# Token blocks of 768, 768 and 576 with seven products in the first two, the low parts of the weights on one engine by kind, and a longer lag before the stores

## The chip, the cores and the metric

The kernel runs on one core of one Trainium2 chip. The metric is the device time of one execution in microseconds, median over the runs. The core has a matrix engine (PE, whose weight loads are shown as PEld), a vector engine (VectorE, DVE in the profile), an activation engine (ScalarE, ACT), a general engine (GpSimd, POOL) and a synchronization engine (SyncE, SP), which issues nearly all DMA transfers. Each engine works off its own instructions in the order in which the program gives them to it; between engines they are held together by semaphores.

## What is computed

One layer of a streaming encoder over 2048 prompt tokens and 64 sample tokens, each a row of 1024 floats, in float32:

```python
h = rms_norm(x, norm1_g) * (1 + sc1) + sh1
z = h @ w_in                       # conv pair | q | k | v | two gates
conv_out = conv_module(...)        # depthwise, 31 taps, LayerNorm, projection
attn_out = attend(q, k, v) @ w_attn_out
merged = sigmoid(g_conv) * conv_out + sigmoid(g_attn) * attn_out
x = x + gt1 * (merged @ w_o)
h2 = rms_norm(x, norm2_g) * (1 + sc2) + sh2
gate, up = split(h2 @ w_ffn_in)    # 1024 -> 2 x 2816
x = x + gt2 * ((silu(gate) * up) @ w_ffn_out)
```

The prompt and the sample have their own conditioning, so their own shifts, scales and gates (`gt1`, `gt2`).

## The kernel before

**Products.** A float32 product is made of three matmuls. Each operand x is kept as two tiles, a high part (x copied to the matrix engine's reduced float type) and a low part (x minus the high part); the matmuls are high by high, high by low, low by high. For every weight tile that comes from memory ACT writes the high part (`whi`), and a subtraction `wlo<-...,whi` writes the low part. That subtraction is on VectorE or on GpSimd: `Weights.split` chooses (lines 458 to 460). Before the change the down weights, the up weights and the merge's weights go to GpSimd, unless the planner's own clock for GpSimd runs more than `BEHIND` = 4000 ns ahead of its clock for PE; then VectorE gets it. Of `w_o` every second slab is always VectorE's.

**Stages.** Up to about 1226 us the kernel makes the projections, the convolution and the attention, in four blocks of tokens (`PBLOCKS`), and leaves conv and attention outputs and the gates in DRAM (`c_d`, `o_d`, `g_d`). What follows runs once for each block of `CBLOCKS`, a loop that starts at line 1720. Before, the blocks have 576, 768 and 768 tokens; the sample's 64 tokens are the first tile of block 0. A block has these steps:

- the merge: the two projections of `c_d` and `o_d` (weights of the kind "ca"), multiplied by the gates, in two chunks of columns;
- `w_o`, the residual `x1`, its norm (`residual`, line 1630: the factor `r` is a power on GpSimd, then ACT scales the row, PE transposes it), and from its columns the operand tiles of the up projection (`t1` to `t4`, `b11` to `b22`, written by VectorE);
- the up projection, `up`, line 1924, over 22 slices f of 128 hidden columns. It works on 2 by 2 blocks (two halves of the contraction, two halves of the tokens) by Winograd's scheme: seven products in place of eight, where sums of weight quarters (`s1` to `s4`, and the plain ones `a11`, `a12`, `a22`) meet sums of token quarters. The first slices are begun earlier with "fi" weights, while the norm is still under way (tile `early`);
- the down projection, accumulated in token rows `acc`; block 0 does it plainly (eight products, "fo" weights, two slices at a time), blocks 1 and 2 do the pairs f = 4, 6, ..., 18 (`PAIRS`) with seven products ("dn" weights, sums T1 to T4 of `w_ffn_out` rows). In up() a callback `at` puts the slabs of a pair of the down projection between those of the next pair of the up projection; `dn_at` says where;
- the end of the block: the last two slices of the down projection for all tiles, multiplied by `gt2` and added to `x1`, then stored. The rows `x1` come from DRAM again (`x<-x_d`).

The sums `s1` to `s4` are made once, in block 0, by GpSimd (`ws<-...`), and are stored to `sum_d`; blocks 1 and 2 load them. Likewise the first block with "dn" makes their sums and their high and low parts and stores these; the other one loads them.

**What sets the order.** The program is written by a planner. Every instruction that passes `Meter.run` (line 104, so nearly all instructions show L104) adds an estimated time to its engine's clock in the planner; generators of side work (weight loads, residuals, stores) are stepped when their due time has come. The order on each engine is thereby fixed in advance, and a store of an output is emitted `OUT_LAG` = 4000 ns after the planner's time of the instruction that wrote it (line 2019). Weights wait in pools: five slabs of `whi` and `wlo` (`held`), three staging tiles `wst`, one `wup`, two `wfo`, four `ws` for sums. In PSUM there are four banks of the tag "y" and four of "gp", of which the down projection's `pd` takes two at a time.

Of the kernel before, what the change touches and what calls it, by code (L numbers as in the profile page):

```python
# [35 lines left out]
CBLOCKS = [(0, 576), (576, 1344), (1344, 2112)]  # L36
# [14 lines left out]
OUT_LAG = 4000.0  # L51
# [28 lines left out]
def tile_chunks(lo, hi):  # L80

    tiles = token_tiles(lo, hi)
    t, n = tiles[(len(tiles) + 1) // 2 - 1]
    return [(lo, t + n), (t + n, hi)]
# [168 lines left out]
class Weights:  # L253
# [5 lines left out]
    def __init__(self, tc, engines, pool, dram, stream, keys, source, staging, held, kept):  # L259
# [17 lines left out]
        for i, key in enumerate(keys):  # L277
            n = times[key] = times.get(key, 0) + 1
            if key[0] == "dn" and n == 1:
# [85 lines left out]
    def kind(key):  # L365
        return "fo" if key[0] in ("fo", "fr") else ""

    def free_tag(self, kind, sure=True):

        tags = self.tags[kind]  # L370
        if kind == "fo" and (self.items[self.due["fo"][0]][0] == "fr" or any(self.items[i][0] == "fi" for i in self.due[""])):
            tags = tags[:1]
# [17 lines left out]
    def load_on(self, kind):  # L390
        while self.due[kind] and self.free_tag(kind):
            self.load(kind)
# [48 lines left out]
    def split(self):  # L441
# [17 lines left out]
        if name == "pool" and self.sum_pool and self.stream.load["pool"] - self.stream.load["pe"] > BEHIND:  # L459
# [81 lines left out]
def up_operands(f):  # L541
# [3 lines left out]
    ops = (["s2", "s3", "s1"] if f else ["s3", "s2", "s1"]) + ["a12"] * (f >= EARLY) + ["a22"] + ["a11"] * (EARLY <= f + 1 < NF) + ["s4"]  # L545
# [3 lines left out]
def dn_at(f):  # L549

    return (0, 1, 3, 6 if f == PAIRS[-1] else 4)
# [8 lines left out]
def weight_order():  # L560
# [10 lines left out]
    for s, (lo, hi) in enumerate(CBLOCKS):  # L571
# [4 lines left out]
        for f in range(0, NF, 2):  # L576
            ops = up_operands(f) + up_operands(f + 1)
            for j in range(0, len(ops), 2):
                yield ("up", *ops[j : j + 2])
                if s and f - 2 in PAIRS:  # L580
# [4 lines left out]
        yield from (("fo", f) for f in range(NF - 2 if s else NF - 4, NF))  # L585
# [3 lines left out]
def streaming_layer(ctx: ExitStack, tc: tile.TileContext, I, O):  # L589
# [479 lines left out]
    def gate_columns(c0, c1, ct):  # L1069
        g = [half_piece(ct % 2, "tg") for _ in range(2)]  # L1070
        for j in range(2):
            nc.sync.dma_start(g[j][:, : c1 - c0], g_d[j, ct, :, c0:c1])
        return g

    def load_mixed(c0, c1, i):

        src = [[quarter("cin", i) for _ in range(2)] for _ in range(2)]
        for j, a in enumerate((c_d, o_d)):
            for l in range(2):
                nc.sync.dma_start(src[l][j][:, :, : c1 - c0].bitcast(F32), a[l, :, :, c0:c1].rearrange("c p t -> p c t"))  # L1080
# [549 lines left out]
    def residual(pp, t, n, gt1, a, half, hs, free, last):  # L1630


        which = int(t < SMP)
        x_t = [wk.tile([P, 512], F32, tag="ws", name="x_t", bufs=4) for _ in range(2)]
        for j in range(2):
            nc.sync.dma_start(x_t[j][:n], rows(x_p, x_s, t, n)[:, 512 * j : 512 * j + 512])
# [83 lines left out]
    for s, (lo, hi) in enumerate(CBLOCKS):  # L1720
        tiles = token_tiles(lo, hi)
        half = (hi - lo) // 2
        gt1, groups, hs = {}, [], None
        chunks = tile_chunks(lo, hi)
        for i, (c0, c1) in enumerate(chunks):
# [8 lines left out]
            if not groups:  # L1734
                for which in {int(t < SMP) for t, _ in tiles}:
# [39 lines left out]
        hid = [wk.tile([P, 2, 2, CW] if not s else [P, 4, 2, CW // 2], F32R, tag="m0", name="hid"), None]  # L1775
# [40 lines left out]
        def rows_of(f, t, n):  # L1816

            if s:
# [5 lines left out]
        def hidden(f, i, ps):  # L1824
            if s:
# [98 lines left out]
        def up(f, ops, at):  # L1924
# [27 lines left out]
            rest_of_late()  # L1952
            if f % 2 == 0:
                at(0)
            step(y, "s1", "t1", False, False)
            plus(v, y, v)
            if f % 2:
                at(4)
            if f >= EARLY:
                x = bank("gp")  # L1960
                step(x, "a12", "b21", True, True)
                plus(x, x, s1)
                silu(c1, x)
            if f % 2 == 0:
# [3 lines left out]
            two = s and f - f % 2 in PAIRS  # L1968
# [15 lines left out]
        def down(fs, ws):  # L1984

            last = fs[-1] == NF - 1
            for i, (t, n) in enumerate(tiles):
# [3 lines left out]
                gt = gt2[int(t < SMP)] if last else None  # L1991
# [12 lines left out]
                for j, ps in enumerate(pss):  # L2004
# [7 lines left out]
                    else:  # L2012
                        if not final:
                            dve.tensor_tensor(ps[:n], ps[:n], dst, ALU.add)
                        dve.tensor_tensor(ps[:n], ps[:n], gt[:n, f], ALU.mult)
                        dve.tensor_tensor(dst, ps[:n], dst if final else x1[j], ALU.add)
                        stream.at(
                            stream.when("dve") + OUT_LAG,
                            lambda t=t, n=n, f=f, dst=dst: nc.sync.dma_start(rows(y_p, y_s, t, n)[:, f], dst),
# [27 lines left out]
        if not s:  # L2047
            W.open("fo", "wfo")
        turns.drain()
# [3 lines left out]
        for f in range(0, NF, 2):  # L2053
            ops = Operands(f)
            if s and f == PAIRS[0]:
                hid[1] = wk.tile([P, 4, 2, CW // 2], F32R, tag="m1", name="hid")
            elif not s and f // 2 % 2 and f >= NF - 4:
                hid[1] = wk.tile([P, 2, 2, CW], F32R, tag="m1", name="hid")

            def at(i, f=f):  # L2060
                if s and f - 2 in PAIRS:
# [10 lines left out]
        end = NF - 2 if s else NF - 4  # L2072
        ws = [W.get(("fo", f)) for f in range(end, NF)]
        gt2 = {which: gt_row(1, which) for which in {int(t < SMP) for t, _ in tiles}}
# [39 lines left out]
```

## Time and profile before

| what | value |
|---|---|
| median of 3 runs | 3046.8 us (3046.7 to 3047.27) |
| the profiled execution's own time | 3042.59 us |
| its span | 3040.8 us |
| DVE busy | 2052.4 us, 67% |
| ACT busy | 1256.8 us, 41% |
| GpSimd (POOL) busy | 985.3 us, 32% |
| instructions | 44889 |
| DMA moved | 690.98 MB, mean 227 GB/s |

The busy shares are means over a long program with unlike stages, so the prediction cuts the span into stretches: the first 1226 us; block 0's start (1226 to 1430), its steady part (1430 to 1726) and its end with block 1's start (1726 to 1946); block 1's steady part (1946 to 2366); its end with block 2's start (2366 to 2566); block 2's steady part (2566 to 3005) and the tail. In rows of groups, "a<-b,c 128x512 x42 | 50.8, 1211" is an instruction that writes tile a from tiles b and c, its shape, its count, the busy time in us and the mean time of one in ns; behind the second bar stands the engine's idle time just before, and what ended it. In rows of the timeline the first two numbers are the start and the duration in us, and a bracket holds the idle time before and its releaser.

### The profile page before, as it was taken

To read this page: it belongs to the slowest core of one execution; us is meant where nothing else is said; L and a number is where in the kernel's file an instruction comes from. 1 tells how busy PE (TensorE), PEld (TensorE's weight loads), DVE (VectorE), ACT (ScalarE), POOL (GpSimd) and SP (SyncE) were. 2 spreads that over 40 slices of the span, in tenths; PEclk is the share of its full clock that TensorE was granted. 3 is DMA by queue.
4 is the path that set the end of the run, shared out by engine and by line. 5 is a ranking of instruction groups with operands and counts; after the bars stand their busy time and mean duration, and the time that the engine had idled before them with its cause. 6 is when DMAs were issued, how large, how long until landed. Compare 5 with 4: busy or idle time off the path is not lost. (4 is left out here: it accounts for less than half of the span.)

```text
span 3040.8 us, 44889 instructions
## 1 busy us (share of the span) xinstructions
PE 2934.8 (97%) x16259; PEld 2606.5 (86%) x16259; DVE 2052.4 (67%) x3835; ACT 1256.8 (41%) x2267; POOL 985.3 (32%) x617
## 2 busy tenths in 40 slices
PE   7989898999999999989999999999999999999998
PEld 4889776888888788878989889999999898999997
DVE  5896678777977895467666755655666756366567
ACT  3324532453254257464444425534444244333332
POOL 1200120101011102355677433247767341333331
PEclk9999998999999999999999999999999999999999
DMA  9888788888997788886444786455556965355554
GB/s 305 268 275 299 230 286 278 275 263 268 305 284 243 247 265 282 253 285 215 149 143 144 231 290 207 157 165 190 182 194 201 342 215 190 118 167 173 166 160 176
DMA packets 487019, 690.98 MB, mean 227 GB/s; under 512 B 38420, under 2 KB 316808, under 8 KB 486797
## 3 DMA queue, kind: packets, MB, share of 16 engines
q1 hardware_dynamic: 474517, 670.72, 67.3%
q10 hardware_dynamic: 12280, 17.39, 1.6%
q8 instruction: 128, 2.10, 0.3%
q14 instruction: 94, 0.77, 0.1%
HBM read 503.79 MB, written 184.19 MB: 226 GB/s over the span
## 5 line engine op out<-in xcount | busy, mean ns | idle before, releaser
L104 POOL TENSOR_TENSOR wlo<-wst,whi 128x1024 fp32r<-128x1024 f32 (+1 forms) x180 | 401.4, 2236 | 491.6 <-ACT whi L104 463.9
L104 PE MATMUL ps<-t,whi 128*128 128x384 f32 (+1 forms) x2112 | 506.1, 324 | 10.0 <-DVE t L104 4.8
L104 PE MATMUL pd<-whi,hid 128*128 128x512 f32 (+1 forms) x1400 | 450.2, 391 | 3.4 <-DVE acc L104 3.4
L104 ACT ACTIVATE whi<-wst 128x1024 fp32r<-128x1024 f32 (+1 forms) x273 | 266.1, 979 | 358.6 <-PE ps L104 123.7
L104 PE MATMUL ps<-b,whi 128*128 128x384 f32 (+1 forms) x1584 | 381.7, 326 | 11.0 <-DVE pw L104 4.0
L104 PEld LDWEIGHTS ps<-t,whi 128*128 128x128 f32 x2112 | 370.7, 189 | 18.4 <-DVE t L104 5.9
L104 DVE SCALAR_TENSOR_TENSOR y<-u,wd,y 128x512 f32<-128x512 f32 (+1 forms) x480 | 369.3, 772 | 6.7
L104 PE MATMUL ps<-hh,whi 128*128 128x512 f32 (+2 forms) x992 | 364.6, 367 | 0.7 <-DVE h L104 0.7
L104 PE MATMUL ps<-hl,whi 128*128 128x512 f32 (+2 forms) x992 | 348.1, 351 | 0.0
L104 PE MATMUL ps<-hh,wlo 128*128 128x512 f32 (+2 forms) x992 | 347.6, 350 | 0.0
L104 DVE TENSOR_TENSOR acc<-acc,pd 128x512 f32<-128x512 f32 (+1 forms) x440 | 290.7, 684 | 80.5 <-PE pd L104 76.9
L104 PE MATMUL ps<-t,wlo 128*128 128x384 f32 (+1 forms) x1056 | 340.8, 323 | 0.0
L104 PEld LDWEIGHTS pd<-whi,hid 128*128 128x128 f32 (+1 forms) x1400 | 258.1, 184 | 64.7 <-DVE acc L104 6.9
L104 PEld LDWEIGHTS ps<-b,whi 128*128 128x128 f32 x1584 | 278.7, 190 | 14.3 <-DVE pw L104 4.3
L104 PE MATMUL pd<-wlo,hid 128*128 128x512 f32 (+1 forms) x700 | 273.7, 391 | 0.0
L104 PE MATMUL ps<-b,wlo 128*128 128x384 f32 (+1 forms) x792 | 257.3, 325 | 0.0
L104 POOL TENSOR_TENSOR r<-t,mhalf 128x8 f32<-128x8 f32 (+3 forms) x68 | 84.4, 1243 | 390.0 <-DVE t L104 380.1
L104 PEld LDWEIGHTS ps<-hh,wlo 128*128 128x128 f32 x992 | 188.6, 190 | 22.7
L104 POOL TENSOR_TENSOR wlo<-wup,whi 128x1024 fp32r<-128x1024 f32 (+1 forms) x64 | 138.2, 2160 | 213.0 <-ACT whi L104 190.7
L104 PEld LDWEIGHTS ps<-hh,whi 128*128 128x128 f32 x992 | 189.3, 191 | 19.7 <-issue 1.9
L104 PEld LDWEIGHTS ps<-hl,whi 128*128 128x128 f32 x992 | 189.3, 191 | 15.5 <-issue 1.4
L104 PEld LDWEIGHTS ps<-t,wlo 128*128 128x128 f32 x1056 | 199.3, 189 | 0.6
(217 smaller groups left out, 5717.5 us busy)
## 6 DMA issues: line engine op xcount, KB each, us to landing
whi<-w_din_h SPq DMA_DIRECT2D x72, 512.0 KB, 5.8
wlo<-w_din_l SPq DMA_DIRECT2D x72, 512.0 KB, 7.0
wst<-sum_d SPq DMA_DIRECT2D x131, 256.0 KB, 2.9
wmod<-in_w_ada SPq DMA_DIRECT2D x48, 512.0 KB, 6.7
sum_d<-ws SPq DMA_DIRECT2D x88, 256.0 KB, 3.2
wst<-in_w_ffn_in SPq DMA_DIRECT2D x85, 256.0 KB, 3.4
wst<-in_w_in SPq DMA_DIRECT2D x40, 512.0 KB, 7.1
wst<-in_w_ffn_in SPq DMA_DIRECT2D x37, 512.0 KB, 5.3
```

Of the source, the lines that this page charges most:

```text
L104: return f(*args, **kw)
```

## The change

Five things are changed.

1. The blocks are 768, 768 and 576 tokens. Blocks 0 and 1 (`SEVEN` = 2) have the seven-product down projection, block 2 the plain one. Inside this stage the sample's tokens are now numbered from `SAT` = 1536, as the first tile of the last block. Loads that cross the seam are cut into pieces (`segments`).
2. The rule with `BEHIND` is gone. The low parts of "dn" slabs are always on VectorE, all others are on GpSimd, but for those that were VectorE's before for good ("in", "qkv", odd `w_o` slabs).
3. At the end of a block VectorE no longer does the third operation, `x1` plus product; GpSimd adds it in place. The last two tiles of the last block keep all on VectorE.
4. The store of an output is emitted 14000 ns after an addition on GpSimd, and 4000 ns after one on VectorE as before.
5. For odd f the product `a12` comes before `s1`, not behind it, in `up` and in the order of the weights; the third "dn" slab of a pair comes one step later. The "dn" rows count as kind "fo" in the staging tiles, and the plain "fo" loads of block 2 are held back until that block opens them.

```diff
-CBLOCKS = [(0, 576), (576, 1344), (1344, 2112)]
+CBLOCKS = [(0, 768), (768, 1536), (1536, 2112)]
+SAT = 1536
...
-OUT_LAG = 4000.0
+OUT_LAG = {"dve": 4000.0, "pool": 14000.0}
...
-BEHIND = 4000.0
+SEVEN = 2
...
+def block_tiles(lo, hi):
+    head = [(SAT, SMP)] if lo == SAT else []
+    return head + [(u, P) for u in range(lo + SMP * len(head), hi, P)]
+
+def stored_at(u):
+    return u if u >= SAT + SMP else u - SAT if u >= SAT else u + SMP
+
+def segments(c0, c1):
+    cuts = [c0] + [c for c in (SAT, SAT + SMP) if c0 < c < c1] + [c1]
+    return [(a - c0, stored_at(a), b - a) for a, b in zip(cuts, cuts[1:])]
...
         e, name = (self.dve, "dve") if key[0] in ("in", "qkv") or key[0] == "wo" and key[1] % 2 else (self.gps, "pool")
-        if name == "pool" and self.sum_pool and self.stream.load["pool"] - self.stream.load["pe"] > BEHIND:
+        if key[0] == "dn":
             e, name = self.dve, "dve"
...
-    ops = (["s2", "s3", "s1"] if f else ["s3", "s2", "s1"]) + ["a12"] * (f >= EARLY) + ["a22"] + ["a11"] * (EARLY <= f + 1 < NF) + ["s4"]
+    ops = (["s2", "s3"] if f else ["s3", "s2"]) + ["a12"] * (f >= EARLY and f % 2) + ["s1"] + ["a12"] * (f >= EARLY and f % 2 == 0) + ["a22"] + ["a11"] * (EARLY <= f + 1 < NF) + ["s4"]
...
-    return (0, 1, 3, 6 if f == PAIRS[-1] else 4)
+    return (0, 1, 3, 6 if f == PAIRS[-1] else 5)
...
+        seven = s < SEVEN
...
                     else:
+                        name = "dve" if hi == T and i >= len(tiles) - 2 else "pool"
                         if not final:
                             dve.tensor_tensor(ps[:n], ps[:n], dst, ALU.add)
-                        dve.tensor_tensor(ps[:n], ps[:n], gt[:n, f], ALU.mult)
-                        dve.tensor_tensor(dst, ps[:n], dst if final else x1[j], ALU.add)
+                        if name == "pool":
+                            dve.tensor_tensor(dst, ps[:n], gt[:n, f], ALU.mult)
+                            stream.after("pool", "dve")
+                            gps.tensor_tensor(dst, dst, x1[j], ALU.add)
+                        else:
+                            dve.tensor_tensor(ps[:n], ps[:n], gt[:n, f], ALU.mult)
+                            dve.tensor_tensor(dst, ps[:n], dst if final else x1[j], ALU.add)
                         stream.at(
-                            stream.when("dve") + OUT_LAG,
+                            stream.when(name) + OUT_LAG[name],
...
         if not s:
             W.open("fo", "wfo")
+        elif not seven:
+            W.limit = 1 << 30
+            W.load_on("fo")
```

The planner turns these edits into another order of instructions. PE keeps the same 16027 instructions, each shape as often as before. VectorE goes from 3837 to 3750, GpSimd from 622 to 709, SyncE from 1908 to 1928. Rows of the first stage move little; the places below are the ones that the prediction speaks of. A row is the line, the operation, written tile, read tiles and shape, and a count where it stands several times in a row.

The first place is GpSimd's queue in the steady part of block 0. Before, in the block of 576, it makes the sums `ws` of the up weights and the low parts of these and of the plain down slabs (`wfo`):

```order
L104 TENSOR_TENSOR ws<-wst 128x512
L104 TENSOR_TENSOR ws<-ws,wup 128x512
L104 TENSOR_TENSOR wlo<-wfo,whi 128x1024
L104 TENSOR_TENSOR ws<-wup,wst 128x512
L104 TENSOR_TENSOR wlo<-wst,whi 128x512
L104 TENSOR_TENSOR wlo<-wup,whi 128x512
L104 TENSOR_TENSOR ws<-wup,ws 128x512
L104 TENSOR_TENSOR ws<-wst 128x512
L104 TENSOR_TENSOR wlo<-ws,whi 128x512 x2
L104 TENSOR_TENSOR ws<-ws,wst 128x512
```

With the change, in the block of 768, the sums of the down rows (`ws<-wfo`) stand in the same queue:

```order
L122 TENSOR_TENSOR wlo<-wst,whi 128x512
L122 TENSOR_TENSOR wlo<-ws,whi 128x512
L122 TENSOR_TENSOR ws<-wfo 128x512
L122 TENSOR_TENSOR wlo<-ws,whi 128x512 x2
L122 TENSOR_TENSOR ws<-wfo 128x512
L122 TENSOR_TENSOR ws<-wfo,ws 128x512
L122 TENSOR_TENSOR wlo<-ws,whi 128x512
L122 TENSOR_TENSOR wlo<-wst,whi 128x512
L122 TENSOR_TENSOR ws<-wfo,ws 128x512
L122 TENSOR_TENSOR ws<-wst,ws 128x512
L122 TENSOR_TENSOR ws<-wst 128x512
```

So both kinds of sums now fall into one block, and the low parts of the down slabs have left the queue for VectorE.

The second place is VectorE's queue while block 1's operand tiles are written, just before its up projection. Before, three low parts of whole weight tiles stand between them:

```order
L104 TENSOR_TENSOR t_19675<-pw,t_19674 128x4x128
L104 TENSOR_TENSOR wlo<-wst,whi 128x1024
L104 TENSOR_SCALAR pw<-pw,A_173,B_174 128x128
L104 TENSOR_TENSOR b_19671<-xn,b_19670 128x4x128
L104 TENSOR_TENSOR pw<-xn,pw 128x512
L104 TENSOR_TENSOR pw<-pw,b_18744 128x512
L104 TENSOR_TENSOR wlo<-wup,whi 128x1024
L104 TENSOR_TENSOR pw<-pw,b_18745 128x512
L104 TENSOR_TENSOR t_19673<-pw,t_19672 128x4x128
```

With the change none of these is left there:

```order
L122 TENSOR_SCALAR pw<-pw,A_173,B_174 128x128
L122 SCALAR_TENSOR_TENSOR early<-tg,ps 128x384
L122 TENSOR_TENSOR pw<-xn,pw 128x512
L122 TENSOR_TENSOR pw<-pw,b_19377 128x512
L122 TENSOR_TENSOR b_20336<-xn,b_20335 128x4x128
L122 TENSOR_TENSOR pw<-pw,b_19378 128x512
L122 TENSOR_TENSOR t_20338<-pw,t_20337 128x4x128
```

The `wlo` rows moved to GpSimd's queue; the tiles `t`, which PE waits for, follow one another.

The third place is the end of a block on GpSimd, with the change (before, no `acc` row stands in its queue). The additions of `x1` (tiles `x_...`) stand between the low parts of the next block's first weights:

```order
L122 TENSOR_TENSOR wlo<-wfo,whi 128x1024 x2
L122 TENSOR_TENSOR wlo<-wst,whi 128x1024 x2
L122 TENSOR_TENSOR acc<-acc,x_18826 128x512 x3
L122 TENSOR_TENSOR acc<-acc,x_18827 128x512 x3
L122 TENSOR_TENSOR acc<-acc,x_18828 128x512 x3
L122 TENSOR_TENSOR acc<-acc,x_18829 128x512 x3
L122 TENSOR_TENSOR wlo<-wst,whi 128x1024
L122 TENSOR_TENSOR wlo<-wup,whi 128x1024
```

Twelve additions come between the second and the third slab of the next merge; on VectorE the rows `acc<-pd,x` of the same places are gone.

More of the change, by code (lines that the diff above doesn't have):

```diff
@@ L584, in weight_order @@
                     yield from (("fo", f - 2), ("fo", f - 1))
-        yield from (("fo", f) for f in range(NF - 2 if s else NF - 4, NF))
+        yield from (("fo", f) for f in range(NF - 2 if s < SEVEN else NF - 4, NF))
 @with_exitstack
@@ L1734, in streaming_layer @@
             if not groups:
-                for which in {int(t < SMP) for t, _ in tiles}:
+                for which in {int(t == SAT) for t, _ in tiles}:
                     gt1[which] = gt_row(0, which)
@@ L1952, in up, with factor @@
             rest_of_late()
+            def factor():
+                if f >= EARLY:
+                    x = bank("gp")
+                    step(x, "a12", "b21", True, True)
+                    plus(x, x, s1)
+                    silu(c1, x)
             if f % 2 == 0:
                 at(0)
+            else:
+                factor()
             step(y, "s1", "t1", False, False)
@@ L1957, in up @@
             if f % 2:
[L1958 to L1964, printed above, removed]
+                at(5)
+            else:
+                factor()
                 at(1)
@@ L1967, in up @@
             plus(z, z, u2)
-            two = s and f - f % 2 in PAIRS
+            two = seven and f - f % 2 in PAIRS
             dve.tensor_tensor(z, z, c1, ALU.mult)
```

47 lines of the change are left out of this document (28 added, 19 removed).

## The prediction

> **What bounds the kernel now.** I read the page's busy times first, then the windows view of core 0 cut at the stages, then the waits and the timeline of the stretches in which PE is not full. The columns of the windows view are the stretch, its length, the busy time of PE, PEld, DVE, ACT and POOL with instruction counts, the granted clock, the DMA share and GB/s.
>
> ```profile
> PE 2934.8 (97%) x16259; PEld 2606.5 (86%) x16259; DVE 2052.4 (67%) x3835; ACT 1256.8 (41%) x2267; POOL 985.3 (32%) x617
> ...
> 1226.00:1430.00 204.00, 187.89 (x1130) 167.90 (x1131) 125.41 (x233) 101.78 (x180) 97.97 (x62) 0.97 0.81 270
> 1430.00:1726.00 296.00, 292.14 (x1870) 267.72 (x1869) 195.85 (x292) 122.09 (x247) 195.84 (x132) 1.00 0.46 147
> 1766.00:1806.00 40.00, 37.22 (x193) 35.18 (x193) 22.56 (x35) 14.19 (x18) 14.16 (x6) 0.96 0.93 318
> 1900.00:1946.00 46.00, 43.43 (x241) 42.17 (x240) 39.09 (x66) 26.50 (x49) 8.56 (x6) 0.96 0.56 199
> 1946.00:2366.00 420.00, 420.00 (x2207) 393.87 (x2207) 241.71 (x415) 185.62 (x309) 260.23 (x149) 1.00 0.55 180
> 2366.00:2406.00 40.00, 37.71 (x184) 32.67 (x183) 31.83 (x55) 8.75 (x12) 11.45 (x5) 1.00 1.07 372
> 2526.00:2566.00 40.00, 37.37 (x200) 34.37 (x199) 33.98 (x59) 28.12 (x53) 4.06 (x4) 0.97 0.57 199
> 3005.00:3041.00 36.00, 26.44 (x121) 21.51 (x119) 28.80 (x49) 1.97 (x4) 0.00 (x0) 0.95 0.57 213
> ```
>
> PE is the bound: 97% busy, and in block 1's steady part (1946 to 2366) without a gap. The change keeps every matmul, so it can only move what is left: the idle time of each stretch, and the clock below 1.00. As idle plus (1 less clock) times length, block 0's start loses 16.1 + 6.1 = 22.2 us, its steady part 3.9, the two stretches of the transition from block 0 to 1 4.4 and 4.4, the transition from 1 to 2 2.3 and 3.8, the tail 9.6 + 1.8 = 11.4. That is 52.4 us, the most that these stretches can give; the first 1226 us are hardly touched and I leave them as they are.
>
> **Block 0's start.** The waits of PE in 1226 to 1430 (who waited for whom: total, times, longest), then the timeline of one of them:
>
> ```profile
> PE ps L104 <- DVE pw L104: 4.0, 1, 4.0
> PE ps L104 <- DVE early L104: 3.6, 1, 3.6
> PE ps L104 <- DVE t L104: 3.1, 3, 1.5
> PE ps L104 <- DVE v L104: 2.8, 2, 1.9
> ...
> 1342.18 5.02 POOL L104 TENSOR_TENSOR wlo<-wst,whi 128x512 fp32r<-128x512 f32 x4
> 1347.14 0.57 POOL L104 TENSOR_TENSOR r<-t,mhalf 128x1 f32<-128x1 f32 x1
> 1347.74 1.15 ACT L104 ACTIVATE xn<-x,r 128x1024 f32<-128x1024 f32 x1 [3.80 <-POOL r L104]
> ...
> 1349.73 0.85 PE L104 MATMUL ps<-b,whi 128*128 128x288 f32 x2 [3.61 <-DVE early L104]
> ```
>
> The factor r of a token tile stands behind four low parts on GpSimd, ACT waits 3.80 us for it, and PE has no more early products to do. A block of 576 tokens gives PE fewer columns for each such step: its early and first up matmuls are 288 wide, those of 768 are 384 wide, 4/3 of the work over which the same weight preparation is spread. The other starts show what a block of 768 loses: 4.4 us in 1900 to 1946 and 3.8 us in 2526 to 2566. But these load ready sums, and block 0 must make its own on GpSimd, so the low parts still stand ahead of r (in the new order two, then three of them in one stretch, in place of four and four, and the third r behind sums that wait for loads). I take 7 us for the stall at r with the clock it costs, and 3 us for the rest: 22.2 goes to 10, **−12**. Bounds: −20 (nearly the loss of 1900 to 1946 alone), and 0 (the first block loses what it did).
>
> **From block 0 to 1.** This is now a passage from 768 to 768, as the one from 1 to 2 was. What PE waited for in the old second stretch, and what stood ahead of it:
>
> ```profile
> 1920.43 1.22 DVE L104 TENSOR_TENSOR wlo<-wst,whi 128x1024 fp32r<-128x1024 f32 x1
> ...
> 1923.68 2.57 DVE L104 TENSOR_TENSOR wlo<-wup,whi 128x1024 fp32r<-128x1024 f32 x1
> ...
> 1926.78 0.67 DVE L104 TENSOR_TENSOR t<-pw,t 128x512 fp32r<-128x512 f32 x1
> ...
> 1922.76 2.41 POOL L104 TENSOR_TENSOR wlo<-wst,whi 128x1024 fp32r<-128x1024 f32 x1 [14.83 <-ACT whi L104]
> 1927.50 0.45 PE L104 MATMUL ps<-t,whi 128*128 128x384 f32 x1 [2.37 <-DVE t L104]
> ```
>
> VectorE wrote two low parts (1.22 + 2.57 = 3.79 us) ahead of the tile t that PE waited 2.37 us for, while GpSimd had stood idle 14.83 us. Without `BEHIND` both go to GpSimd, and t comes up to 3.79 us sooner: the 2.37 us go, with the 1.8 us of lower clock that followed. What stays is a residue like that of the first stretch of the old second passage, 2 us: 8.8 to 2, **−6.8**. Bounds −8.8 (all) and 0: on GpSimd a slab of 1024 takes 2.41 us in place of 1.22, so the slab, not t, may be late next.
>
> **From block 1 to 2**, now from 768 to 576. At the block's end VectorE does three operations for each half tile, and PE waits for the bank:
>
> ```profile
> 2388.45 0.50 PE L104 MATMUL pd<-whi,hid 128*128 128x512 f32 x1 [0.57 <-DVE acc L104]
> ...
> 2399.21 0.62 PE L104 MATMUL ps<-cin,whi 128*128 128x384 f32 x2 [0.57 <-DVE acc L104]
> ```
>
> Two operations in place of three end these waits, so 2.3 goes to 0. In exchange GpSimd gets 12 additions. I put one at 1.3 us, the mean of its other 128x512 operations in block 1 (1292 ns, below): 15.5 us, with the low parts of the next merge slabs queued behind, and each addition waits for its VectorE product and the load of `x1`. Up to five slabs are ready ahead, and GpSimd had 11.45 us of work in those 40 us, so I let the cover hold; if it is gone, a merge slab is up to 15 us late. In the second stretch the block of 576 brings its narrow columns: of the row list of block 0's start I carry the waits for pw and v over, 4.0 + 2.8, and 3.8 goes to 7. Sum **+1**, bounds −4 and +15.
>
> **The steady parts.** Groups by shape, the first four of block 0 (1430 to 1726), the next three of block 1 (1946 to 2366); the last two rows, of the chain, show one period of block 1's pairs:
>
> ```profile
> L104 DVE TENSOR_TENSOR wlo<-ws,whi 128x512 fp32r<-128x512 f32 x42 | 50.8, 1211 | 5.5 <-ACT whi L104 3.3
> L104 POOL TENSOR_TENSOR wlo<-wst,whi 128x512 fp32r<-128x512 f32 x26 | 39.6, 1530 | 0.3
> L104 POOL TENSOR_TENSOR wlo<-ws,whi 128x512 fp32r<-128x512 f32 x24 | 34.0, 1427 | 63.3 <-ACT whi L104 63.3
> L104 POOL TENSOR_TENSOR ws<-wst 128x512 f32<-128x512 f32 x20 | 29.6, 1478 | 17.8 <-DMA wst<-in_w_ffn_in 13.9 <-DVE acc L104 3.2 <-POOL wlo L104 0.4
> ...
> L104 POOL TENSOR_TENSOR wlo<-ws,whi 128x512 fp32r<-128x512 f32 x32 | 41.0, 1292 | 13.2 <-ACT whi L104 13.0
> L104 POOL TENSOR_TENSOR ws<-wfo 128x512 f32<-128x512 f32 x14 | 18.4, 1316 | 33.5 <-DMA wfo<-in_w_ffn_out 33.5
> L104 DVE TENSOR_TENSOR acc<-acc,pd 128x512 f32<-128x512 f32 x175 | 114.7, 684 | 19.0 <-PE pd L104 17.4
> ...
> 2066.21 12.60 PE ps L104 x72
> ...
> 2110.08 12.60 PE ps L104 x72
> ```
>
> A pair of slices in a block of 768 takes PE 2110.08 − 2066.21 = 43.87 us. In the new block 0 GpSimd must do in it, by the order, 8 sums and 14 low parts for the up weights and 4 sums for the down rows: 26 operations of 128x512. At 1292 ns that is 33.6 us, at 1530 ns 39.8 us; both fit into 43.87. VectorE's load is 241.71 / 420 of its time in block 1, 25.2 us of a pair, plus 7 low parts at 0.684 to 1.211 us, 4.8 to 8.5: 30 to 34 us. Neither engine is full, but the queues are in order and linked: a down sum on GpSimd, its copy on ACT, its low part on VectorE, the next use of one of four `ws` tiles. Waits of GpSimd for ACT and loads came to 63.3 + 17.8 us over the old 296. So I give the new first block 5 us of loss, and 1 us for the block of 576 (3.9 before, with VectorE's 42 low parts in it): 3.9 to 6, **+2**. Bounds: −4 (none of it lost), and +40, the rival below.
>
> A rule of the Trainium skill speaks against this part: its page "SBUF — State Buffer", section "Who interferes with whom", says that a VectorE instruction with two inputs in SBUF and a GpSimd instruction on SBUF exclude each other, so that the second stands until the first is done. The rows agree so far as the same VectorE subtraction of 1024 elements took 1.22 us and 2.57 us, the long one with GpSimd at work. By the rule each VectorE low part would take its own time from GpSimd, at most 7 of 0.68 us = 4.8 us a pair, an estimate, and 33.6 + 4.8 = 38.4 us still fits.
>
> **The tail.** PE's last matmul, and the chain behind it:
>
> ```profile
> 3032.74 0.39 PE L104 MATMUL pd<-whi,hid 128*128 128x512 f32 x1
> ...
> 3032.96 2.48 DVE acc L104 x4
> 3035.44 1.21 DVE pd L104 x2
> 3036.64 0.59 DVE acc L104
> ```
>
> From the end of the last matmul (3033.13) to 3040.8 pass 7.7 us, since VectorE, with six operations for a tile, is the slower one there: it comes to the end with work left. With four operations for all tiles but the last two it does not lag until then. Three PE waits of 0.57 us go, and of the 2.48 us of `acc` at the head the part that belongs to the tile before, with about a microsecond of clock; I take **−5**. Bounds −5.5 and −2 (the last two tiles alone bring the lag back). The longer lag before the stores costs nothing on this path: only the last two tiles' stores stand behind the end, and they keep 4000 ns. Twenty more loads by SP, and the changed places of `a12` and the third down slab, I put at nothing; their cover is the slabs held ready, and without it each costs a wait like PE's 0.57 us.
>
> **Sum**: −12 − 6.8 + 1 + 2 − 5 = −20.8 on the profiled execution's 3042.6, so 3021.8. The median of the runs lies 4.2 us above that execution, so **3026 us**.
>
> **Rivals.** *GpSimd becomes the bound of the new block 0* (slower). It decides from the point where its cycle passes 43.87 us: 26 operations at 1530 ns are 39.8 us; if some 9 us of waits for ACT, for loads and for a free `ws` come on top in each pair, 48.8 − 43.9 = 4.9 us in each of 8 pairs, 39 us. The 5 us that the sum holds for it become 39: 3026 + 34 = 3060. For it speaks the 63.3 us that the queue waited for ACT; against it that it waited while it was ahead of need, since PE lost only 3.9 us. Chance 0.18.
>
> *Block 0's start keeps its loss*, because it comes from preparing weights in the same order, not from narrow columns: −12 becomes 0, 3026 + 12 = 3038. For it speaks that low parts still stand ahead of r; against it that PE has 4/3 of the work to bridge them. Chance 0.17.
>
> *The start's loss follows the block of 576 to the end*: the late merge slabs behind 15.5 us of additions, +15 in place of +1, so 3040; with a part of the first rival on top no change. Chance 0.12. My forecast has the rest, 0.53.
>
> **How the numbers follow.** The forecast's own range is 3012 to 3038, from the terms' bounds taken half way. The range holds the two smaller rivals and most of the way to the first: 3010 to 3053. A measurement of this kernel tells a difference from about 0.2%, 6 us. Faster than 3040.7: the forecast nearly whole (0.50), the second rival mostly (0.13), the third by half (0.06), so 0.69; within 6 us 0.12; slower 0.19, the first rival with a little of the others.
>
> **What would show it.** In the new profile PE in 1226 to about 1440 should lose near 10 us in place of 22, no `wlo` from `wst` or `wup` of 1024 should stand on VectorE between the tiles t before block 1's up projection, and the period of the pairs in block 0 should be 43.9 us with GpSimd at 34 to 40 of it. A period of 45 us or more, with PE waiting for `whi` or `wlo`, is the first rival. A gap of several us in the merge of block 1 or 2 that ends with GpSimd's `wlo` would show that the additions were not covered. The tail after the last matmul should be under 5 us. If VectorE, not GpSimd, holds PE in the steady part of block 0, my 30 to 34 us were too small.

## The result, and the profile after

The changed kernel takes 3075.76 us (median of 4 runs, 3074.85 to 3080.68) against 3047.03 us for the kernel before (median of 4, 3046.7 to 3049.13). The ratio is 1.010, with a 95% interval of 1.0088 to 1.0112: slower by about 29 us, where 3026 was forecast. The profiled execution is the longest of the four, 3080.68 us with a span of 3078.9 us.

The windows view of the kernel after, cut where block 0's merge begins (1224.5) and then at each first down product and each next merge. The columns are those of the prediction's view (stretch, length, busy time of PE, PEld, DVE, ACT, POOL, granted clock, DMA share, GB/s):

```profile
1224.50:1423.70 199.20, 189.71 (x984) 175.18 (x985) 105.89 (x187) 94.52 (x158) 106.36 (x69) 0.98 0.76 256
1423.70:1905.70 482.00, 454.69 (x2305) 414.89 (x2305) 299.01 (x495) 194.42 (x378) 329.31 (x248) 0.99 0.56 191
1905.70:2113.40 207.70, 192.99 (x986) 177.51 (x985) 109.66 (x188) 88.29 (x139) 79.21 (x40) 0.95 0.68 226
2113.40:2555.40 442.00, 442.00 (x2306) 412.65 (x2305) 255.50 (x439) 157.78 (x257) 172.09 (x77) 1.00 0.54 172
2555.40:2714.20 158.80, 150.05 (x929) 136.39 (x928) 89.32 (x179) 76.80 (x130) 75.76 (x38) 0.97 0.78 258
2714.20:3078.90 364.70, 359.81 (x2246) 326.29 (x2244) 154.41 (x289) 135.89 (x220) 200.32 (x88) 1.00 0.44 136
```

The kernel before, cut at the same places:

```profile
1226.30:1394.30 168.00, 153.10 (x928) 137.81 (x929) 102.44 (x194) 84.57 (x149) 79.30 (x48) 0.96 0.82 268
1394.30:1760.50 366.20, 361.43 (x2246) 326.19 (x2245) 244.87 (x371) 146.36 (x289) 217.60 (x147) 1.00 0.55 180
1760.50:1954.00 193.50, 188.14 (x986) 174.79 (x985) 116.66 (x196) 88.15 (x139) 64.17 (x33) 0.98 0.66 225
1954.00:2399.20 445.20, 442.92 (x2305) 411.74 (x2303) 261.86 (x449) 188.93 (x313) 265.05 (x152) 1.00 0.59 196
2399.20:2588.50 189.30, 186.66 (x985) 173.74 (x986) 116.10 (x199) 86.31 (x137) 57.33 (x28) 0.99 0.67 224
2588.50:3040.80 452.30, 442.94 (x2305) 411.75 (x2303) 266.50 (x457) 153.61 (x253) 151.51 (x64) 1.00 0.49 161
```

With idle time plus (1 less clock) times length, as in the prediction, PE's loss by stage is:

| stage | before | after | forecast change | change |
|---|---|---|---|---|
| block 0's start | 21.6 | 13.5 | −12 | −8 |
| block 0, steady | 4.8 | 32.1 | | +27 |
| block 0 to 1 | 9.2 | 25.1 | −6.8 | +16 |
| block 1, steady | 2.3 | 0 | | −2 |
| block 1 to 2 | 4.5 | 13.5 | +1 | +9 |
| block 2 and the tail | 9.4 | 4.9 | −5 | −4.5 |
| sum | 51.8 | 89.1 | −20.8 | +37 |

(The three steady rows together were forecast at +2.) The sum, +37.3, agrees with the spans, 3078.9 − 3040.8 = +38.1. The medians differ by 28.7 only: the profiled execution before lies 4.4 us below its median, the one after 4.9 us above, so some 9 us of the table is scatter between executions. The counts of matmuls say the same without a formula: blocks 0 and 1 of the new kernel have the same 2305 matmuls in their steady parts, and block 0 takes 482.0 us for them, block 1 442.0, without a gap.

**Where block 0 loses it.** The waits of GpSimd and of PE in block 0's steady part (who waited for whom: total in us, times, longest):

```profile
POOL wlo L122 <- ACT whi L122: 61.3, 30, 10.6
POOL ws L122 <- DMA sum_d<-ws: 37.2, 8, 6.2
POOL ws L122 <- DVE wlo L122: 37.0, 23, 2.5
```

```profile
PE pd L122 <- DVE acc L122: 21.0, 14, 2.6
PE pd L122 <- DVE s L122: 5.0, 7, 3.4
```

Eight times, once a pair, GpSimd waits for a store of a sum to `sum_d`. One of them in the timelines of GpSimd, SP, ACT, VectorE and PE, one row or two of each:

```profile
1651.97 1.29 POOL L122 TENSOR_TENSOR wlo<-ws,whi 128x512 fp32r<-128x512 f32 x1
1657.90 1.29 POOL L122 TENSOR_TENSOR ws<-ws,wst 128x512 f32<-128x512 f32 x1 [4.63 <-DMA sum_d<-ws]
...
1650.78 0.38 SPq L402 DMA_DIRECT2D wup<-in_w_ffn_in  x1
1651.22 0.57 SPq L402 DMA_DIRECT2D wst<-in_w_ffn_in  x1
1651.85 7.68 SPq L451 DMA_DIRECT2D sum_d<-ws  x3
...
1659.22 0.63 ACT L122 ACTIVATE whi<-ws 128x512 fp32r<-128x512 f32 x1 [4.35 <-POOL ws L122]
...
1660.26 0.56 DVE L122 TENSOR_TENSOR hid<-ps,hid 128x384 fp32r<-128x384 f32 x1 [4.40 <-ACT hid L122]
...
1661.56 0.47 PE L122 MATMUL pd<-whi,hid 128*128 128x512 f32 x1 [1.90 <-DVE acc L122]
...
1662.52 1.29 DVE L122 TENSOR_TENSOR wlo<-ws,whi 128x512 fp32r<-128x512 f32 x2
```

GpSimd may write the next sum only when a store has freed its `ws` tile, and stands still for 4.63 us. ACT stands behind the sum's high part for 4.35 us, with a `hid` in its queue; VectorE waits 4.40 us for that `hid`, with `acc` additions behind it; PE waits for the bank that these free. The row that names PE's releaser shows VectorE, three steps from the cause.

Two things lie behind this wait. The store left late: GpSimd had written its sum by 1648.15, but SP, in whose queue two weight loads stand ahead, issued it no sooner than 1651.85. And two of the four `ws` tiles are closed to the up sums meanwhile: T1 and T2, which GpSimd began to write at 1635.58 and 1638.21, are read by VectorE's low parts only at 1662.52, in the last row.

**Where the passages lose it.** At the end of block 0, SP, GpSimd, ACT and PE:

```profile
1895.00 15.19 SPq L2057 DMA_DIRECT2D out<-acc  x12
1910.28 1.53 SPq L1095 DMA_DIRECT2D tg<-g_d  x2
1911.86 0.42 SPq L402 DMA_DIRECT2D wst<-in_w_attn_out  x1
...
1907.28 2.55 POOL L122 TENSOR_TENSOR acc<-acc,x 128x512 f32<-128x512 f32 x2 [0.18 <-DVE acc L122]
1917.10 2.36 POOL L122 TENSOR_TENSOR wlo<-wst,whi 128x1024 fp32r<-128x1024 f32 x1 [7.27 <-ACT whi L122]
...
1915.97 1.05 ACT L122 ACTIVATE whi<-wst 128x1024 fp32r<-128x1024 f32 x1
...
1917.07 1.33 PE L122 MATMUL ps<-cin,whi 128*128 128x384 f32 x3 [2.72 <-ACT whi L122]
```

SP's queue holds twelve stores that follow GpSimd's additions one by one, 15.19 us, and the next merge's gates and weights are issued only behind them. GpSimd itself is free by then: after its last addition it stands idle for 7.27 us, until ACT has a high part ready. Before, the stores of this place took little more than half as long, and weights of the merge stood ahead of them:

```profile
1762.12 8.29 SPq L2019 DMA_DIRECT2D out<-acc  x10
```

The lag of 14000 ns does not change this. With 4000, 14000 or 100000 the program has the same order on every engine: the planner's `flush` at the end of the block writes out whatever is left. The fourth edit does nothing.

At the end of block 1, SP, VectorE and PE of the changed kernel:

```profile
2560.23 8.25 SPq L2057 DMA_DIRECT2D out<-acc  x12
...
2573.80 0.49 DVE L122 SCALAR_TENSOR_TENSOR t<-tg,ps 128x320 f32<-128x320 f32 x1 [9.14 <-DMA tg<-g_d]
...
2574.44 0.87 PE L122 MATMUL ps<-cin,whi 128*128 128x320 f32 x2 [4.79 <-DVE t L122]
```

Here the stores take no longer than before (8.15 us for twelve), but the gates `tg` are again issued behind them, and PE's largest wait, 4.79 us, ends with these.

### The profile page after: what moved, and what is told of

The parts are those of the page before. It is cut to its first block, busy times and chain, and to the rows that moved or that the text cites. A ratio compares the mean times of both kernels' runs of the same rounds, so it can differ in the third digit from the quotient of the medians.

```text
span 3078.9 us, 44859 instructions
## 1 busy us (share of the span) xinstructions
PE 2947.8 (96%) x16259; PEld 2615.0 (85%) x16259; DVE 1956.3 (64%) x3748; ACT 1256.9 (41%) x2267; POOL 1115.9 (36%) x704
## 5 line engine op out<-in xcount | busy, mean ns | idle before, releaser
L122 POOL TENSOR_TENSOR wlo<-wst,whi 128x1024 fp32r<-128x1024 f32 (+1 forms) x216 | 459.0, 2131 | 523.2 <-ACT whi L122 466.7
L122 POOL TENSOR_TENSOR wlo<-wup,whi 128x1024 fp32r<-128x1024 f32 (+1 forms) x68 | 144.9, 2132 | 165.4 <-ACT whi L122 135.1
L122 PEld LDWEIGHTS ps<-hl,whi 128*128 128x128 f32 x992 | 189.8, 191 | 15.5 <-issue 1.4
```

What stands on the lines that cost most here:

```text
L122: return f(*args, **kw)
```

## The experiments

Three theories for block 0: A, the `ws` tiles are too few; B, GpSimd is too slow for its operations; C, the low parts of the down slabs on VectorE tie three engines together. Two for the passages: S, the stores hold up SP's queue; G, GpSimd's additions delay the low parts behind them.

**e1: the changed kernel without the stores to `sum_d`.** The two later blocks read other data in their place.

```diff
-            self.stream.at(
-                self.stream.when("pool"), lambda j=j, t=t: self.sync.dma_start(self.sum_d[f][j], t), True
-            )
...
-                sum_d[f][int(op[1]) - 1] if op[0] == "s"
+                w_fo[f * P : f * P + P, 512 * (int(op[1]) % 2) : 512 * (int(op[1]) % 2) + 512].rearrange("p (k n) -> p k n", k=4) if op[0] == "s"
```

> The changed kernel without the stores of the up sums to sum_d in block 0; blocks 1 and 2 load pieces of w_ffn_out of the same size in their place, so their up products are of other numbers. Theory A (tiles ws): in each pair of block 0 GpSimd waits some 4.6 us for a store of ws to land before it may write the next sum, and that wait is what PE loses: the period falls from about 49.5 us to about 44 to 45.5 and the time by 25 to 40 us, to about 3036 to 3050. Theory B (GpSimd is too slow for 26 operations a pair): its operations are the same, so the period stays above 48 us and the time within 8 us of 3076. Theory C (the low parts of the down slabs on VectorE link three engines in order): no more than a third of the loss goes, 3062 or above.

Measured 3051.55 us, ratio to the kernel before 1.0015 (1.0004 to 1.0027). Block 0's steady part in the windows view:

```profile
1422.70:1882.00 459.30, 449.77 (x2306) 410.77 (x2306) 297.74 (x495) 195.05 (x378) 331.22 (x248) 1.00 0.47 158
```

and GpSimd's largest waits in it:

```profile
POOL wlo L122 <- ACT whi L122: 59.2, 32, 10.6
POOL ws L122 <- DVE wlo L122: 51.5, 23, 4.1
```

482.0 falls to 459.3, more than half of the 40 us, so the stores are one part of it (without them SP's queue is shorter too). The other stays: a `ws` tile with a down sum is freed only by VectorE's low part, and the waits for that rise from 37.0 to 51.5 us. GpSimd's work is the same 331 us; B is excluded as the main cause.

**e2: the four down sums on VectorE.**

```diff
-                self.gps.tensor_tensor(t, x, y, ALU.subtract)
+                self.dve.tensor_tensor(t, x, y, ALU.subtract)
```

> The changed kernel with the four sums T of a pair of down rows on VectorE, 22 operations instead of 26 on GpSimd. Theory B: 4 x 1.3 = 5.2 us a pair come off GpSimd, the period falls below 45.5 us, the time by 25 to 40 us. Theory A: as many ws tiles are in use and the store lands as late; the wait stays, on GpSimd or now on VectorE, and the time changes by less than 12 us, or rises. Theory C: GpSimd no longer waits for VectorE's low parts (34.7 us in all over block 0), some 10 to 25 us go.

Measured 3056.62 us, 1.003 (1.0018 to 1.0042). The time alone would have fitted C, but the stretches place it elsewhere:

```profile
1427.30:1905.70 478.40, 453.59 (x2305) 413.33 (x2304) 319.67 (x527) 196.19 (x379) 289.77 (x217) 0.99 0.57 193
1905.70:2096.90 191.20, 186.64 (x986) 173.77 (x985) 106.90 (x188) 86.86 (x138) 77.18 (x39) 0.99 0.73 244
```

GpSimd is busy 290 us in place of 329 and block 0 gains 3.6 us: it was not the amount of its work. Its waits for the stores stay, 33.1 us in eight. The 16.5 us (207.7 to 191.2) come from the passage to block 1, whose order the planner wrote differently; what in that order pays is not shown.

**e3: the low parts of the down slabs back on GpSimd.**

```diff
-        if key[0] == "dn":
-            e, name = self.dve, "dve"
```

> The changed kernel with the low parts of the down slabs back on GpSimd: 33 operations a pair, 42.6 us at 1.29 us, of 43.87. Theory B: GpSimd is over-full, the period rises to 50 to 55 us, the time by 10 to 45 us. Theory A: the ws wait of 4.6 us comes on top of a full queue, so slower as well, by 10 to 45 us. Theory C: faster by 10 us or more, since the waits of GpSimd for VectorE are gone.

Measured 3088.7 us, 1.0131 (1.0107 to 1.0155). Block 0's steady part takes 495.4 us. C's gain does not come: with VectorE's part the stretch is some 13 us shorter. The test is not a clean one, since GpSimd carries 391 us of work here in place of 329.

**e4: T1 and T4 written over the row quarters that they read last.** This version computes everything, with the same operations.

```diff
-        return ((o, o), (e, o), (), (o,))[key[2]]
+        return ((o,), (e, o), (e,), (o,))[key[2]]
...
+                if name in ("T1", "T4"):
+                    t = {"T1": blocks.get("B12"), "T4": blocks.get("B21")}[name]
+                else:
+                    t = self.sum_pool.tile([P, 4, P], F32, tag="ws", name="ws", bufs=4)
+                    t = t.rearrange("p a b -> p (a b)").unsqueeze(1)
```

> The changed kernel with the sums T1 and T4 written over the row quarters they are the last to read, so a pair uses two ws tiles for them and not four; the number of operations on each engine is the same. Theory A: with 10 tiles a pair through the four buffers in place of 12 the store has more time to land, the period falls by 2 to 5 us and the time by 15 to 40 us. Theory B: the same work on GpSimd, within 8 us of 3076. Theory C: within 10 us.

Measured 3035.19 us, 0.9963 (0.9952 to 0.9975), below the kernel before. The steady part of block 0:

```profile
1426.40:1868.60 442.20, 442.20 (x2306) 412.46 (x2305) 310.30 (x495) 195.58 (x378) 335.28 (x248) 1.00 0.61 209
```

and GpSimd's largest waits in it:

```profile
POOL wlo L122 <- ACT whi L122: 63.3, 23, 10.4
POOL ws L122 <- DVE wlo L122: 23.8, 8, 3.4
```

No wait for a store is left, and the block runs without a gap although GpSimd is as busy as before (335 us) and still waits 63.3 us for ACT. This settles A: two tiles a pair fewer, one of them the long-held T1, 40 us less. It excludes C too, since VectorE still writes the low parts of the down slabs. (More `ws` buffers in place of this were not tried. Nor was the fifth edit undone, which puts the third "dn" slab, the one with T1 and T2, a step later; whether it lengthens their hold is open.)

**e5: as e4, with stores that really leave late** (they are kept out of `flush` but for the last block's).

```diff
                             lambda t=t, n=n, f=f, dst=dst: nc.sync.dma_start(rows(y_p, y_s, stored_at(t), n)[:, f], dst),
+                            hi < T,
```

> As e4 (sums T1 and T4 in place, 3035.2 us), and the stores of the outputs of blocks 0 and 1 really leave with the lag: they go into SP's queue when the planner's clock has passed it, among the loads of the next merge, and not all together at the end of the block. The loss of PE between the last down product of block 0 and the first of block 1 was 22.6 us in e4, and 10.6 us from block 1 to 2. Theory S (twelve stores that wait for GpSimd's additions hold up SP's queue, with the merge's weights and gates behind them): these fall to 8 to 14 and 5 to 8 us, the time to 3020 to 3029. Theory G (the twelve additions themselves, 15.5 us of GpSimd, delay the low parts behind them): no change, within 4 us of 3035.

Measured 3019.47 us, 0.9921 (0.9897 to 0.9945). The two passages:

```profile
1868.80:2064.30 195.50, 188.42 (x985) 174.96 (x984) 110.19 (x188) 88.76 (x139) 79.57 (x40) 0.97 0.71 238
...
2506.40:2653.70 147.30, 146.21 (x930) 132.82 (x929) 89.11 (x179) 76.56 (x130) 75.93 (x38) 1.00 0.84 278
```

206.0 falls to 195.5 us and 155.7 to 147.3 (from e4), with the additions still on GpSimd: S, not G, as GpSimd's idle 7.27 us above had it for the first passage.

**e6: as e4, with the additions of x1 back on VectorE.**

```diff
-                        name = "dve" if hi == T and i >= len(tiles) - 2 else "pool"
+                        name = "dve"
```

> As e4, with the additions of x1 back on VectorE in all tiles (three operations a half tile, the stores still together at the end of the block). Both S and G: the two passages lose less, 22.6 to 9 to 14 us, 10.6 to 5 to 9 us; the time after the last matmul goes back from 4.6 to 7.7 us and the 0.57 us waits of PE return, 5 us in the tail. Together 3024 to 3033.

Measured 3029.99 us, 0.9953 (0.9937 to 0.997), as expected in sum, and the passages take 198.4 and 150.0 us. One part missed: the time behind the last matmul did not go back. The tail of e6, in the chain that ended last, is as short as the changed kernel's, 4.6 us from PE's end (3026.65) to the end of the span (3031.2):

```profile
2999.79 26.86 PE pd L122 x118
...
3027.40 0.69 DVE acc L122
```

**e7: as e4, with the rule of before for the low parts** (but the down slabs'). **e8: the kernel before with GpSimd's additions alone.** The edit of e7:

```diff
-        if key[0] == "dn":
+        if key[0] == "dn" or name == "pool" and self.sum_pool and self.stream.load["pool"] - self.stream.load["pe"] > 4000.0:
```

> As e4, with the rule of before for the low parts of all but the down slabs: VectorE takes one when the planner's clock for GpSimd is 4000 ns ahead of PE's. If GpSimd's own load sets what is left in block 0 (theory B in a smaller measure), it is faster by 3 us or more. If VectorE's low parts in front of the tiles t are what the prediction's second term says, the passage from 0 to 1 gets worse by 4 to 9 us. I expect the second: 3036 to 3044.

Measured 3033.63 us, 0.9964 (0.9949 to 0.998), the same as e4. Neither expectation holds by stage: the passage from 0 to 1 is shorter by 12.3 us (206.0 to 193.7), not longer; the one from 1 to 2 is longer by 4.7 (155.7 to 160.4), block 0's steady part by 3.6 (442.2 to 445.8). The first fits S: in the order of e7 SP issues the merge's first weights ahead of the twelve stores, which then take 9.54 us, and PE has no wait for weights left in that passage.

In e8 the third operation of before is done as in the changed kernel:

```diff
-                        dve.tensor_tensor(ps[:n], ps[:n], gt[:n, f], ALU.mult)
-                        dve.tensor_tensor(dst, ps[:n], dst if final else x1[j], ALU.add)
+                        if not (hi == T and i >= len(tiles) - 2):
+                            dve.tensor_tensor(dst, ps[:n], gt[:n, f], ALU.mult)
+                            stream.after("pool", "dve")
+                            gps.tensor_tensor(dst, dst, x1[j], ALU.add)
...
```

> The kernel before with one part of the change alone: GpSimd adds x1 at the end of the blocks, all but the last two tiles of the last block. Theories S and G: both passages between blocks lose 4 to 10 us more each, the tail gains 5 us: 3050 to 3062. If the additions are covered, as the prediction had it, only the gain is left: 3040 to 3043.

Measured 3046.18 us, 1.0 (0.9991 to 1.0009): no change, and neither case. By its stretches one passage is the same (192.9 us against 193.5), the other loses 7.1 us (196.4 against 189.3); block 1's steady part and the last stretch with the tail gain 7.7 (441.7 against 445.2, 448.1 against 452.3).

**e9: the changed kernel with the late stores alone.** The edit is that of e5.

> The changed kernel with the late stores alone (the down sums in ws as changed). If the two causes are apart and add up, block 0's steady part still loses about 40 us, and the passages 10 us and 5 to 10 us less, as from e4 to e5: 3055 to 3063. If the late stores help only where GpSimd has room, less than 6 us is gained: 3069 or above.

Measured 3060.26 us, 1.0055 (1.0039 to 1.0071): 15.5 us less than the changed kernel, where e4 and e5 differ by 15.7 (against the kernel before as measured beside each, 14 and 13 us). The two causes are apart and add up; block 0's steady part still takes 478.0 us.

**e10: as e5, with x_t loaded through ACT's queue.** In e5 one stall was left, before block 1's up projection.

```diff
-            nc.sync.dma_start(x_t[j][:n], rows(
+            nc.scalar.dma_start(x_t[j][:n], rows(
```

> As e5, with the loads of x for the residual (x_t) issued from ACT's queue. In e5 the last stall before block 1's up projection is 4.16 + 2.48 us behind ACT's and VectorE's t; its chain goes back to x_t, whose load stood in SP's queue behind a weight load that waited for a low part on GpSimd. If that queue is the cause, the stall goes or halves: the loss from block 0 to 1 falls from 12.2 to 4 to 8 us, the time to 3010 to 3016. If ACT itself is the late engine there (weight copies of 1.06 us between the parts of the last tile), the stall stays and the time is within 4 us of 3019.5, or above it if ACT stands still for a free ws tile.

Measured 3019.56 us, 0.9924 (0.9905 to 0.9943). The stall is there to the hundredth. PE's and ACT's timelines in e10:

```profile
2030.03 0.69 PE L122 MATMUL ps<-t,whi 128*128 128x384 f32 x1 [4.16 <-ACT t L122]
2033.19 0.69 PE L122 MATMUL ps<-t,whi 128*128 128x384 f32 x1 [2.48 <-DVE t L122]
...
2027.89 1.08 ACT L122 ACTIVATE whi<-wst 128x1024 fp32r<-128x1024 f32 x1
2028.83 0.65 ACT L122 ACTIVATE b<-xn 128x512 fp32r<-128x512 f32 x1
2029.35 0.62 ACT L122 ACTIVATE t<-pw 128x512 fp32r<-128x512 f32 x1
```

and GpSimd's and VectorE's in the changed kernel, around the same stall:

```profile
2081.99 2.34 POOL L122 TENSOR_TENSOR wlo<-wst,whi 128x1024 fp32r<-128x1024 f32 x1 [0.70 <-ACT whi L122]
...
2071.74 0.68 DVE L122 TENSOR_TENSOR b<-xn,b 128x512 fp32r<-128x512 f32 x1
...
2082.46 2.42 DVE L122 TENSOR_TENSOR b<-xn,b 128x512 fp32r<-128x512 f32 x1
```

The queue of x_t is excluded. PE's first wait ends with ACT's `t`, which stands behind a weight copy of 1.08 us; its second with VectorE's `t`, which stands behind a `b` of 2.42 us that took 0.68 elsewhere.

**e11: as e5, with the additions of x1 on VectorE** (the edit of e6).

> As e5, with the additions of x1 back on VectorE. What is left of GpSimd's additions as an advantage once the stores are out of the way: the tail's 5 us, and three PE waits of 0.57 us at each block's end. By that 3024 to 3031; if VectorE's third operation costs nothing between blocks, 3020 to 3024.

Measured 3026.31 us, 0.9943 (0.9928 to 0.9959). With the stores out of the way GpSimd's additions seem to be worth 6.8 us; the intervals of e5 and e11 overlap, so this rests on the stretches. It is not the tail that pays (4.6 us behind the last matmul in both), but the ends of blocks 0 and 1: the steady parts that hold them take 445.7 and 445.5 us, 442.3 and 442.1 in e5.

**e12: as e5, with the rule back** (the edit of e7).

> As e5, with the rule of before back (VectorE takes a low part, but of the down slabs always, when the planner's clock for GpSimd is 4000 ns ahead). In e7 the stall before block 1's up projection was 2.41 us with the rule, where e4 had 4.16 + 2.48. If the removal of the rule is what makes that stall, the loss from block 0 to 1 falls from 12.2 to 4 to 8 us, while block 0's pairs lose some 3 us more on VectorE (6.8 instead of 3.2, as in e7): 3015 to 3020. If not, the loss stays at 9 to 13 us and the time is 3020 to 3026.

Measured 3020.03 us, 0.9918 (0.9902 to 0.9935). The passage from 0 to 1 falls from 195.5 to 189.0 us, so the rule's removal made most of that stall (2.42 + 0.72 us are left of 4.16 + 2.48); block 0's steady part pays 3.5 us (442.3 to 445.8), the passage from 1 to 2 5.4 (147.3 to 152.7). Nothing is left in sum. e5, e10 and e12 cannot be told apart; each is about 25 us faster than the kernel before.

## Why the prediction was wrong

**The steady parts (+2, measured +25).** This step failed. It counted GpSimd's operations, 26 at 1.29 to 1.53 us, and put 5 us on "in order and linked" queues. The operations did fit: e4 has as many and no gap. What was not counted was the room: with both kinds of sums in one block, twelve sums a pair pass through four `ws` tiles, eight of them held until a store has landed and four until VectorE's low part is done. The sign that the prediction set for the first rival, PE waiting for `whi` or `wlo`, did not come either: PE waited for VectorE's `acc`, 21.0 us, though VectorE was busy for 299 of the 482 us only. The rival priced at 39 us (chance 0.18) named "waits for ACT, for loads and for a free `ws`" and gave the right size, 40 us; but its title, GpSimd as the bound, was wrong, as e2 and e4 show, so that the size fitted was luck, and the largest wait that spoke for it, GpSimd's for ACT (63.3 us), is harmless: e4 has 63.3 us of it too.

**From block 0 to 1 (−6.8, measured +16).** Two steps failed. The additions' price was looked for in GpSimd's queue and in the weights' low parts, and put in the passage from 1 to 2 only; what they delay is SP's queue, through the stores (e5: −10.5 us here). And the two low parts taken from VectorE did not end the wait for t. On GpSimd they run beside VectorE's `b`, and PE waited 4.16 + 2.48 us in place of 2.37; with the rule back (e12) the passage is 6.5 us shorter. How much of this is VectorE's longer `b`, and how much ACT's place in the new order, no run tells apart.

**From 1 to 2 (+1, measured +9).** Inside the bounds, but not by the late merge slab that the upper bound stood for: the gates came late behind the same stores. Without them in the way (e5) the passage loses 1.1 us, less than before's 4.5. The additions have a part in it, since on VectorE (e6) the passage is 5.7 us shorter with the stores still together; how they act, where the stores take no longer than before, is not shown. The narrow columns of the block of 576 cost nothing there.

**Block 0's start (−12, measured −8).** Right in sign, a third too large. PE's wait for `early`, the one behind r, fell from 3.6 to 0.5 us, in the direction forecast; new waits for ACT's `t` (4.6 us) and `xn` (2.2 us) took part of the gain. That it was the wider columns, no run shows by itself.

**The tail (−5, measured −4.5).** Right in size, for the wrong reason. The prediction gave it to the third operation; e6 has that operation back and the same 4.6 us behind the last matmul. The plain down projection of the last block ends with four slices for a tile in place of two, and between VectorE's groups of operations in the tail it now waits for PE, where before PE waited for it. What the third operation gains lies at the ends of the two other blocks (e11).

**"The longer lag costs nothing."** True, since the lag does nothing; and had it worked it would have been worth 15.5 us (e9). The prediction followed the stores only to the kernel's end, not past the other two block ends, where SP's queue goes on.

With both faults mended (e5) the loss of PE is 12.5 + 12.9 + 1.1 + 5.0 = 31.5 us, 20.3 less than before: the forecast's −20.8, but with the passage from 0 to 1 worse and that from 1 to 2 better than it said, so the agreement of the sums is luck.

## What to carry to other kernels

When two preparations are moved into the same stage, count the buffers that they share and how long each is held, stores included, before adding up the busy time of the engine that does them. An engine with 68% busy time can be the first cause of a stall that the waits of the bound engine put down to a third one: follow the waits from engine to engine until one ends with a DMA. When the last operation before a store moves to another engine, look at the queue that issues the store, and at what stands behind it; and see whether a constant that is changed reaches the order of instructions at all.

## What the runs showed of the hardware

VectorE's operations with two inputs in SBUF can be longer beside GpSimd, those with one input in PSUM are not. In block 0's steady part of the changed kernel the groups of the same subtraction, by shape:

```profile
L122 DVE TENSOR_TENSOR wlo<-wfo,whi 128x512 fp32r<-128x512 f32 x24 | 26.1, 1086 | 3.9 <-ACT whi L122 3.7
L122 DVE TENSOR_TENSOR wlo<-ws,whi 128x512 fp32r<-128x512 f32 x32 | 24.2, 775 | 11.0 <-ACT whi L122 11.0
```

Of these 56, the 25 that no GpSimd operation overlaps take 0.69 us, the other 31 take 1.09 us on average and up to 1.80; `acc<-acc,pd`, with one input in PSUM, takes 0.68 us whether GpSimd works or not. The `b` of 2.42 us above began 1.87 us before the end of a GpSimd subtraction and took 1.74 us longer than the other. This is what the Trainium skill says on the page "SBUF — State Buffer", section "Who interferes with whom": the one that comes second waits until the first is done. The prediction weighed that rule for GpSimd's loss alone, where it hardly mattered (e4 runs without a gap); here it shows in the other direction, on VectorE's short operations in front of the matmuls. What that cost in time was not separated from ACT's late `t`.
